# Attention with queries on rows: key sums as backward scans on VectorE, weights transposed on TensorE, own keys and values of two heads in one tile, gating and the final norm rearranged

## The chip, the cores and the metric

The kernel runs on one core of one Trainium2 chip. The metric is the time of one execution on the device in microseconds (us); where several executions are compared, their median. In the lines of the profile, PE is TensorE (PEld its weight loads), DVE is VectorE, ACT is ScalarE, POOL is GpSimd, SP is SyncE, which here only issues transfers.

## The reference, cut to what matters

Two request groups (256 new frames, and 64 further frames of a stream that has 256 cached keys and values) go through one layer with shared weights. All of it is float32.

```python
xn = rmsnorm(x, norm_mix)
q, k, v, u, vs, g = split(xn @ w_in)            # 8 heads x 128; 8 gating groups x 128
z = einsum('bqhd,bkhd->bhqk', q, k) * 128 ** -0.5
mask = k_pos[None, :] < q_pos[:, None]
log_stay = where(mask, log_sigmoid(-z), 0.0)
log_rest = cumsum(log_stay, axis=3, reverse=True) - log_stay
w = where(mask, exp(log_sigmoid(z) + log_rest), 0.0)
a = einsum('bhqk,bkhd->bqhd', w, v)             # sample group: k, v = cached rows, then its own
vs = rmsnorm(gelu(vs), sgu_norm)
bb = gelu(u) * (spatial mix of vs in 128-position chunks + b_spatial)
h = x + (sigmoid(g_a) * (a @ w_a) + sigmoid(g_b) * (bb @ w_b)) @ w_out
hn = rmsnorm(h, norm_ffn)
h = h + (silu(hn @ w_gate) * (hn @ w_up)) @ w_down
y = rmsnorm(h, norm_final)                      # outputs: y, k, v, and vs of the sample rows
```

The sum runs over the keys from the last one backwards. With softplus sp(z) = -log_sigmoid(-z), the weight of a key is exp(z - sum of sp over this key and all later ones).

## The kernel before, in words

**Layout.** Features lie on the 128 partitions, and the 320 positions (256 prompt, 64 sample) along the free dimension. Each large product is done as three float32r products: the weight tile is split into a rounded part `wh` (ScalarE, L75) and a rest `wl` (VectorE, L76), the activations likewise, and `product` (L80 to L85) issues hi*hi, hi*lo and lo*hi for each 128x128 weight block.

**The weight pipeline.** `block` (L87) computes 128 output features: it takes the weights in halves of 8 blocks (1024 columns). A half, here called a chunk, is one transfer of 512 KB issued by SP, one `wh`, one `wl` and 24 matmuls of 320 columns. The pool has 3 raw buffers and 4 pairs of split buffers, so the `wh` of a chunk can only be written when TensorE has finished the chunk four before it, and the transfer of a chunk waits for the `wl` of the chunk three before it. After each chunk a counter, the tick, advances, and functions that were booked for that tick (`at`) put their instructions into the program there. So the attention and gating work is strewn between the chunks of the projections. Each engine runs its own queue in order; which instruction stands where on ScalarE, VectorE and GpSimd is decided when the program is built.

**Attention, in pairs of heads.** `attend` (L442) books for each pair of heads: scores two ticks after its last projection, `att_values` at 4, `att_sums` at 6, `att_out` of the two heads at 9 and 10. Keys lie on the partitions of the score tiles, queries along the free dimension. `att_scores` computes k^T q in full float32 (10 matmuls), copies them out of PSUM with the mask added, and makes the softplus of two tiles of 512 and 640 columns: Abs, Exp, Ln on ScalarE, one VectorE instruction, then a hi and lo split. `att_sums` gets the sums over later keys as products with a triangle and a block of -1 (12 float32r matmuls on `sph` and `spl`), adds the scores and takes Exp. `att_values` transposes v to keys on partitions (6 transposes), and `att_out` multiplies (5 matmuls for each head). The scratch tiles z and e of 640 columns come from the pool of 8 tiles named `D`.

**Gating.** For each of 8 groups: `sgu_turn` scales by the norm and transposes (3 transposes), two ticks later `sgu_mix` does three float32 matmuls with the mask of the chunk, adds the bias and multiplies by u.

**The end.** After the last `w_down` product, L573 adds it to h, L582 squares it, six one-column matmuls (L590) sum the squares of all features, ScalarE takes a square root, VectorE refines the reciprocal in five small instructions (L593, L154 to L157) and writes three diagonal matrices (L598); three matmuls (L599) spread them over all partitions, 16 VectorE instructions (L601) scale the output and 9 transfers (L605) write it.

Of the kernel before, what the change touches and what calls it, by code (L numbers as in the profile page):

```python
# [8 lines left out]
F32 = mybir.dt.float32  # L9
F32R = mybir.dt.float32r  # L10
# [3 lines left out]
P = 128  # L14
# [19 lines left out]
def stream_step(ctx: ExitStack, tc: tile.TileContext, xT, w_in, w_a, w_b, w_out, w_gu, w_down,  # L34
# [93 lines left out]
    def t320(tag, bufs=2, dt=F32):  # L128
# [15 lines left out]
    neg1 = const.tile([P, P], F32, name="neg1")  # L144
    nc.gpsimd.memset(neg1, -1.0)
    negt = const.tile([P, P], F32, name="negt")
    nc.gpsimd.affine_select(out=negt, in_=neg1, pattern=[[-1, P]], base=0, channel_multiplier=1,
                            compare_op=ALU.is_ge, fill=0.0)
    neg1r = const.tile([P, P], F32R, name="neg1r")
    negtr = const.tile([P, P], F32R, name="negtr")  # L150

# [137 lines left out]
    for o, i in ((neg1r, neg1), (negtr, negt)):  # L289
        tc.keep_in_program_order(nc.vector.tensor_copy(o, i))  # L290
# [6 lines left out]
    bsb = apool.tile([P, H, P], F32, name="bsb")  # L297

    def gate_load():
        tc.keep_in_program_order(nc.sync.dma_start(out=wst.rearrange("p g t -> p (g t)"), in_=ws_t))  # L300
        nc.gpsimd.memset(wst[64:128, :, 0:64], 0.0)

    def bias_load():
# [5 lines left out]
    KT1, S0, NA = 512, 768, 1152  # L309
    mask0 = apool.tile([P, 256], F32, name="mask0")  # L310
    nc.gpsimd.memset(mask0, 0.0)

    nc.gpsimd.affine_select(out=mask0, in_=mask0, pattern=[[1, 256]], base=0,
                            channel_multiplier=-1, compare_op=ALU.is_gt, fill=NEG)

    mask2 = apool.tile([P, 64], F32, name="mask2")
    nc.gpsimd.memset(mask2, 0.0)
    nc.gpsimd.affine_select(out=mask2, in_=mask2, pattern=[[1, 64]], base=64,
                            channel_multiplier=-1, compare_op=ALU.is_gt, fill=NEG)
    nc.gpsimd.memset(mask2[0:64, :], NEG)  # L320

    def heads(t, n):
        return t.rearrange("p (h t) -> p h t", h=n)

    def att_load(p):
        s = attn[p]
        s["ck"] = apool.tile([P, 2, PAST], F32, tag="ck", name="ck")
        tc.keep_in_program_order(nc.sync.dma_start(out=s["ck"].rearrange("p h t -> p (h t)"),
                                                   in_=ck_t[:, 2 * p * PAST : (2 * p + 2) * PAST]))
        s["cv"] = apool.tile([P, 2, 2, P], F32, tag="cv", name="cv")  # L330
        tc.keep_in_program_order(nc.sync.dma_start(out=s["cv"].rearrange("p i h d -> p i (h d)"),
                                                   in_=cv[:, :, 2 * p * P : (2 * p + 2) * P]))

    def att_scores(p):
        s = attn[p]
        z0, z1 = aux(), aux()
        zs = [aux(), aux()]
        for j in range(2):
            q, k = s["q", j], s["k", j]
            nc.tensor.matmul(z0[:, j * 256 : (j + 1) * 256], k[:, 0:128], q[:, 0:256], start=True, stop=True)  # L340
            nc.tensor.matmul(z1[:, j * P : (j + 1) * P], k[:, 128:256], q[:, 128:256], start=True, stop=True)
            for i in range(3):
                kk = s["ck"][:, j, i * P : (i + 1) * P] if i < 2 else k[:, 192:320]
                nc.tensor.matmul(zs[j][:, i * P : (i + 1) * P], kk, q[:, 192:320], start=True, stop=True)  # L344
        zm = (pair("zm0")[:, 0:KT1], pair("zm1"))
        for j in range(2):
            nc.vector.tensor_tensor(out=zm[0][:, j * 256 : (j + 1) * 256], in0=z0[:, j * 256 : (j + 1) * 256],
                                    in1=mask0, op=ALU.add)
            nc.vector.tensor_tensor(out=zm[1][:, j * P : (j + 1) * P], in0=z1[:, j * P : (j + 1) * P],
                                    in1=mask0[:, :P], op=ALU.add)  # L350
            to = zm[1][:, 256:].rearrange("p (i h t) -> p i h t", i=3, h=2)[:, :, j, :]
            of = zs[j][:, 0:384].rearrange("p (i t) -> p i t", i=3)[:, :, 64:128]
            nc.vector.tensor_copy(to[:, 0:2, :], of[:, 0:2, :])
            nc.vector.tensor_tensor(out=to[:, 2, :], in0=of[:, 2, :], in1=mask2, op=ALU.add)

        hi = apool.tile([P, NA], F32R, tag="sph", name="sph")
        lo = apool.tile([P, NA], F32R, tag="spl", name="spl")
        for z, r in zip(zm, (slice(0, KT1), slice(KT1, NA))):
            e = pair("e")[:, : r.stop - r.start]
            nc.scalar.activation(out=e, in_=z, func=AF.Abs)  # L360
            nc.scalar.activation(out=e, in_=e, func=AF.Exp, scale=-1.0)
            nc.scalar.activation(out=e, in_=e, func=AF.Ln, bias=1.0)  # L362
            nc.vector.scalar_tensor_tensor(out=e, in0=z, scalar=0.0, in1=e, op0=ALU.max, op1=ALU.add)
            nc.scalar.copy(out=hi[:, r], in_=e)
            nc.vector.tensor_tensor(out=lo[:, r], in0=e, in1=hi[:, r].bitcast(F32), op=ALU.subtract)
        s["zm"], s["sp"] = zm, (hi, lo)

    def att_sums(p):

        s = attn[p]  # L370
        zm = s["zm"]
        c0, c1, c2 = aux(), aux(), aux()
        c0b = heads(c0, 2)[:, :, 128:256]
        for i, sp in enumerate(s["sp"]):
            a, b = i == 0, i == 1
            nc.tensor.matmul(c0, negtr, sp[:, 0:KT1], start=a, stop=False)
            nc.tensor.matmul(c0b, neg1r, heads(sp[:, KT1:S0], 2), start=False, stop=b)
            nc.tensor.matmul(c1[:, 0:256], negtr, sp[:, KT1:S0], start=a, stop=b)
            nc.tensor.matmul(c2[:, 128:512], negtr, sp[:, S0:NA], start=a, stop=False, skip_group_check=True)
            nc.tensor.matmul(c2[:, 128:384], neg1r, sp[:, S0 + P : NA], start=False, stop=False, skip_group_check=True)  # L380
            nc.tensor.matmul(c2[:, 128:256], neg1r, sp[:, S0 + 2 * P : NA], start=False, stop=b, skip_group_check=True)
        w0, w1 = zm
        nc.vector.tensor_tensor(out=w0, in0=c0, in1=w0, op=ALU.add)
        nc.scalar.activation(out=w0, in_=w0, func=AF.Exp)
        nc.vector.tensor_tensor(out=w1[:, 0:256], in0=c1[:, 0:256], in1=w1[:, 0:256], op=ALU.add)
        nc.vector.tensor_tensor(out=w1[:, 256:], in0=c2[:, 128:512], in1=w1[:, 256:], op=ALU.add)
        nc.scalar.activation(out=w1, in_=w1, func=AF.Exp)


    own = {}  # L390
    for name, r in (("att", slice(0, 64)), ("sgu", slice(64, P))):
        own[name] = [apool.tile([P, P], F32, name=f"own_{name}{i}") for i in range(2)]
        for t in own[name]:
            nc.gpsimd.memset(t[r, :], 0.0)

    def turned(src, spans, kind, i):

        pt = aux()
        for k, (t0, n) in enumerate(spans):
            nc.tensor.transpose(pt[:n, k * P : (k + 1) * P], src[:, t0 : t0 + n], ident)  # L400
        vn = apool.tile([P, 2, P], F32, tag="vn", bufs=2, name="vn")
        nc.scalar.copy(out=vn.rearrange("p i d -> p (i d)"), in_=pt[:, 0:256])
        o, r = own[kind][i % 2], slice(64, P) if kind == "att" else slice(0, 64)
        nc.scalar.copy(out=o[r, :], in_=pt[r, 256:384])
        return vn, o

    def att_values(p):
        s = attn[p]
        s["vn"] = [turned(s["v", j], ((0, P), (P, P), (192, P)), "att", j) for j in range(2)]

    def att_out(p, j):
        s = attn[p]
        (w0, w1), (vn, own_v), cvt = s["zm"], s["vn"][j], s["cv"]
        po = aux1()

        lo = 256 - 64 * j
        for i in range(3):
            v = cvt[:, i, j, :] if i < 2 else own_v
            nc.tensor.matmul(po[:, lo : lo + P], v, w1[:, 256 + i * P : 256 + (i + 1) * P],  # L419
                             start=i == 0, stop=i == 2)  # L420
        nc.tensor.matmul(po[:, 0:256], vn[:, 0, :], w0[:, j * 256 : (j + 1) * 256], start=True, stop=False)  # L421
        nc.tensor.matmul(po[:, 128:256], vn[:, 1, :], w1[:, j * P : (j + 1) * P], start=False, stop=True)
        aT[2 * p + j] = split("B", po[:, 0:T])
# [238 lines left out]
```

## Time and profile before

| what | value |
|---|---|
| time, median of 3 runs | 1727.84 us (1725.51 to 1728.11) |
| the profiled execution | 1727.79 us, of which 1726.1 us are the span from first to last instruction |
| mean granted TensorE clock | 0.996 |
| busy share | PE 99%, DVE 50%, ACT 39%, POOL 2% |
| mean transfer rate | 152 GB/s |

The page gives for each group of instructions the line, the engine, what is written from what, the count, the busy time in us, the mean time of one in ns, and the idle time of the engine just before them with what ended it. The chain of waits lists, in order of time, the work that set the end: start, length, what. There a matmul counts with the time until the next one starts; in the timeline it counts from its start to the end of its last column, so neighbours overlap. A full float32 matmul appears as two records (`x2`).

### The profile page before, as it was taken

What the parts mean: (1) busy time and instruction counts of PE and PEld (TensorE: products, weight loads), DVE (VectorE), ACT (ScalarE), POOL (GpSimd) and SP (SyncE); (2) the same over time, 40 slices, a digit from 0 to 9 for tenths busy, and PEclk for the clock granted to TensorE, in tenths of its full rate; (3) what the DMA queues carried; (4) which work ended last, traced back from release to release, by engine and by line L of the source; (5) the groups of instructions that cost most, each with busy time, mean ns of one, the idle gap of its engine ahead of it and who ended that gap; (6) DMA issues with size and microseconds to landing.
All of it is one profiled execution on the core that took longest, in us unless ns stands there. A gap on an engine that the chain in (4) does not pass through costs nothing.

```text
span 1726.1 us, 27576 instructions
## 1 busy us (share of the span) xinstructions
PE 1711.0 (99%) x11670; PEld 1708.0 (99%) x11670; DVE 857.2 (50%) x1087; ACT 677.8 (39%) x838; POOL 40.8 (2%) x66
## 2 busy tenths in 40 slices
PE   9999999999999999999999999999999999999997
PEld 9999999999999999999999999999999999999997
DVE  6654446544444445555444444444444444444455
ACT  6554464433333333444333332233333322333342
POOL 0000011000000000110000000000000000000000
PEclk9999999999999999999999999999999999999998
DMA  7454434344444445554444445444444544444453
GB/s 248 161 179 147 158 127 149 128 153 147 149 153 151 147 149 168 175 169 147 150 154 148 148 151 153 147 147 152 153 147 148 154 151 147 149 155 149 129 152 110
DMA packets 79612, 263.20 MB, mean 152 GB/s; under 512 B 8960, under 2 KB 14080, under 8 KB 79488
## 3 DMA queue, kind: packets, MB, share of 16 engines
q1 hardware_dynamic: 78048, 258.25, 46.1%
q0 software_dynamic: 1024, 2.89, 0.5%
q8 instruction: 91, 1.49, 0.3%
q10 hardware_dynamic: 416, 0.31, 0.1%
q14 instruction: 33, 0.27, 0.0%
HBM read 255.90 MB, written 5.51 MB: 151 GB/s over the span
## 4 chain that ended last, share of the span: by engine, by line
PE 98%; ACT 1%; DVE 1%; DMA 0%; issue 0%; ACTq 0%; DVEq 0%
PE acc L84 31%; PE acc L83 31%; PE acc L85 31%; PE aux L227 2%; PE acc L227 1%; DVE h L601 0%; PE aux L419 0%; PE aux L400 0%; PE aux L344 0%; DMA raw<-w_in 0%; PE aux L421 0%; PE aux L340 0%; ACT L471 0%; ACT L362 0%; DVE wl L76 0%; ACT wh L75 0%
## 5 line engine op out<-in xcount | busy, mean ns | idle before, releaser
L75 ACT CAST wh<-raw 128x1024 fp32r<-128x1024 f32 x468 | 484.4, 1035 | 971.5 <-PE acc L84 801.8
L76 DVE TENSOR_TENSOR wl<-raw,wh 128x1024 fp32r<-128x1024 f32 x468 | 565.1, 1208 | 511.1 <-ACT wh L75 508.5
L83 PE MATMUL acc<-A,wh 128*128 128x320 f32 x2464 | 764.1, 310 | 0.0
L85 PE MATMUL acc<-A,wl 128*128 128x320 f32 x2464 | 761.5, 309 | 0.5 <-DVE wl L76 0.5
L84 PE MATMUL acc<-A,wh 128*128 128x320 f32 x2464 | 761.3, 309 | 0.0
L85 PEld LDWEIGHTS acc<-A,wl 128*128 128x128 f32 x2464 | 462.5, 188 | 0.7 <-DVE wl L76 0.7
L83 PEld LDWEIGHTS acc<-A,wh 128*128 128x128 f32 x2464 | 462.6, 188 | 0.2
L84 PEld LDWEIGHTS acc<-A,wh 128*128 128x128 f32 x2464 | 462.6, 188 | 0.2
L85 PE MATMUL acc<-B,wl 128*128 128x320 f32 x960 | 296.6, 309 | 0.0
L83 PE MATMUL acc<-B,wh 128*128 128x320 f32 x960 | 296.6, 309 | 0.0
L84 PE MATMUL acc<-B,wh 128*128 128x320 f32 x960 | 296.6, 309 | 0.0
L83 PEld LDWEIGHTS acc<-B,wh 128*128 128x128 f32 x960 | 180.2, 188 | 0.0
L84 PEld LDWEIGHTS acc<-B,wh 128*128 128x128 f32 x960 | 180.2, 188 | 0.0
L85 PEld LDWEIGHTS acc<-B,wl 128*128 128x128 f32 x960 | 180.2, 188 | 0.0
L83 PE MATMUL acc<-mh,wh 128*128 128x320 f32 x256 | 79.1, 309 | 0.0
L84 PE MATMUL acc<-ml,wh 128*128 128x320 f32 x256 | 79.1, 309 | 0.0
L85 PE MATMUL acc<-mh,wl 128*128 128x320 f32 x256 | 79.1, 309 | 0.0
L563 DVE TENSOR_TENSOR bb<-acc,rh 128x320 f32<-128x320 f32 x44 | 21.6, 492 | 57.8 <-PE acc L85 57.8
L560 DVE TENSOR_TENSOR ev<-acc,rh 128x320 f32<-128x320 f32 x44 | 21.6, 492 | 56.3 <-PE acc L85 56.3
L573 DVE TENSOR_TENSOR h<-acc,h 128x320 f32<-128x320 f32 x48 | 23.5, 489 | 49.9 <-PE acc L85 49.9
L83 PEld LDWEIGHTS acc<-mh,wh 128*128 128x128 f32 x256 | 48.1, 188 | 0.0
L84 PEld LDWEIGHTS acc<-ml,wh 128*128 128x128 f32 x256 | 48.1, 188 | 0.0
(196 smaller groups left out, 768.0 us busy)
## 6 DMA issues: line engine op xcount, KB each, us to landing
raw<-w_gu SPq DMA_DIRECT2D x176, 512.0 KB, 3.5
raw<-w_in SPq DMA_DIRECT2D x141, 512.0 KB, 3.6
raw<-w_down SPq DMA_DIRECT2D x80, 512.0 KB, 3.5
raw<-w_out SPq DMA_DIRECT2D x32, 512.0 KB, 3.6
raw<-w_a SPq DMA_DIRECT2D x16, 512.0 KB, 3.5
raw<-w_b SPq DMA_DIRECT2D x16, 512.0 KB, 3.5
raw<-w_down SPq DMA_DIRECT2D x16, 256.0 KB, 2.7
xr<-xT SPq DMA_DIRECT2D x16, 160.0 KB, 2.6
```

What stands on the lines that cost most here:

```text
L75: nc.scalar.copy(out=wh[:, : n * P], in_=raw[:, : n * P])
L76: nc.vector.tensor_tensor(out=wl[:, : n * P], in0=raw[:, : n * P], in1=wh[:, : n * P].bitcast(F32), op=ALU.subtract)
L83: nc.tensor.matmul(ps[:, :T], a, x[0], start=first, stop=False)
L84: nc.tensor.matmul(ps[:, :T], a, x[1], start=False, stop=False)
L85: nc.tensor.matmul(ps[:, :T], b, x[0], start=False, stop=last)
L227: nc.tensor.matmul(first[b][h][:, :T], w[:, (h * n + j) * P : (h * n + j + 1) * P], xs[c + j][i], start=not last and c + j + i == 0, stop= ...
L560: nc.vector.tensor_tensor(out=t, in0=pg, in1=got["rh"], op=ALU.mult)
L563: nc.vector.tensor_tensor(out=u, in0=pu, in1=got["rh"], op=ALU.mult)
L573: nc.vector.tensor_tensor(out=hs[m], in0=ps, in1=hs[m], op=ALU.add)
```

## The change

- **Scores.** Queries now lie on the partitions, keys along the free dimension. Scores of the prompt are two matmuls for each head (128 and 256 columns); the 64 sample queries of the two heads are put on partitions 0 to 63 and 64 to 127 of one tile by two matmuls of 320 columns with 64 stationary columns. The cached keys are loaded behind the own keys into one tile `k` (`att_keys`), the cached values by `att_rows`, two ticks after the scores.
- **Sums.** The softplus is no longer split. Six `tensor_tensor_scan` instructions on VectorE (L367) run backwards over 128, 256, 128, 256, 64 and 256 columns; the last starts from the value of the one before. Then z minus the sum, and Exp. `att_sums` with its 12 matmuls is gone, and so are its constants.
- **Turning.** `att_turn`, eight ticks after the scores, transposes 14 blocks of 128x128: four of v, one with the sample values of both heads (`vo`, gathered by two GpSimd copies), and nine of weights. Three ScalarE and two VectorE instructions copy them out.
- **Output.** `att_out` for a pair comes four ticks later: one matmul with the own keys of both heads, four of 64 columns with the cached values, and 256 and 128 columns for each head.
- **Gating** works on pairs of groups: five transposes and five matmuls for two groups (before six and six); the 64 sample positions of both share a tile and a block-diagonal weight tile `wso`, which two GpSimd transfers fill.
- **The end.** The last addition, square and sum are done in two pieces (192 and 128 columns); three one-column matmuls instead of six; GpSimd takes the power -0.5 of three columns; three matmuls with a broadcast of these columns replace the diagonals. `busy` puts 6 and 4 matmuls, whose result is not used, before and behind the one-column matmuls. The last transfer is cut into two.

```diff
+        for j in range(2):
+            nc.tensor.matmul(za[j][:, 0:P], q[:, j, 0:P], k[:, j, 0:P], start=True, stop=True)
+            nc.tensor.matmul(za[j][:, P:Z], q[:, j, P:TP], k[:, j, 0:TP], start=True, stop=True)
+        for j, r in enumerate(ROWS):
+            nc.tensor.matmul(zs[r, 0 : KT - TP], q[:, j, TP:T], k[:, j, TP:KT], start=True, stop=True)
...
+        for j, lo, hi, begin in ((0, 0, P, 0.0), (0, P, Z, 0.0), (1, 0, P, 0.0), (1, P, Z, 0.0),
+                                 (1, Z, Z + TS, 0.0), (0, Z, Z + PAST, es[1][:, Z : Z + 1])):
+            back = es[j][:, lo:hi][:, ::-1]
+            nc.vector.tensor_tensor_scan(out=back, data0=ones[:, 0:1].broadcast_to([P, hi - lo]), data1=back,
+                                         initial=begin, op0=ALU.mult, op1=ALU.add)
+        for zz, e in zip(z, es):
+            nc.vector.tensor_tensor(out=zz, in0=zz, in1=e, op=ALU.subtract)
...
-        for i, sp in enumerate(s["sp"]):
-            a, b = i == 0, i == 1
-            nc.tensor.matmul(c0, negtr, sp[:, 0:KT1], start=a, stop=False)
...
+        for i in range(4):
+            nc.tensor.transpose(cols(bv, i), v[:, i // 2, i % 2 * P : (i % 2 + 1) * P], ident)
+        nc.tensor.transpose(cols(ba, 3), s["vo"], ident)
+        for j, b in enumerate((ba, bb)):
+            for i in range(3):
+                nc.tensor.transpose(cols(b, i), cols(z[j], i), ident)
+        for i in range(2):
+            nc.tensor.transpose(cols(bs_, i), cols(z[0], 3 + i), ident)
+        nc.tensor.transpose(cols(bs_, 2), wown, ident)
...
+        mm(po[0][:, TP : TP + P], av[:, 4 * P :], wt[:, 2 * Z + 2 * P :], True, False)
+        for j, r in enumerate(ROWS):
+            for i in range(2):
+                lo = 2 * Z + i * P + j * TS
+                mm(po[0][:, TP + j * TS : TP + (j + 1) * TS], cvt[:, i, j, :], wt[:, lo : lo + TS], False, i == 1)
+        for j in range(2):
+            mm(po[j][:, 0:TP], av[:, 2 * j * P : (2 * j + 1) * P], wt[:, j * Z : j * Z + TP], True, False)
+            mm(po[j][:, P:TP], av[:, (2 * j + 1) * P : (2 * j + 2) * P], wt[:, j * Z + TP : (j + 1) * Z], False, True)
...
         at(now + 2, att_scores, p)
-        at(now + 4, att_values, p)
-        at(now + 6, att_sums, p)
-        at(now + 9, att_out, p, 0)
-        at(now + 10, att_out, p, 1)
+        at(now + 4, att_rows, p)
+        at(now + 10, att_turn, p)
+        at(now + 14, att_out, p)
...
+                for r in PIECES:
+                    keep(nc.vector.tensor_tensor(out=hs[m][:, r], in0=ps[:, r], in1=hs[m][:, r], op=ALU.add))
+                    nc.scalar.activation(out=last[:, r], in_=hs[m][:, r], func=AF.Square)
+                for r in PIECES:
+                    keep(nc.vector.tensor_tensor(out=last[:, r], in0=last[:, r], in1=sqf.total[:, r], op=ALU.add))
...
+    busy(6)
     ps = aux1()
     for t0, c in spans:
+        keep(nc.tensor.matmul(ps[:, c], last[:, t0 : t0 + P], ones[:, 0:1], start=True, stop=True))
...
+    nc.gpsimd.tensor_tensor(out=r, in0=ms, in1=mhalf, op=ALU.pow)
+    busy(4)
...
+        keep(nc.tensor.matmul(rf[:, t0 : t0 + P], r[:, c].to_broadcast([P, P]), ident, start=True, stop=True))
```

VectorE, softplus of the first pair before: `zm` are the masked scores, `e` the softplus, `spl` its rest for the sums, `wl` the rest of a weight chunk, `v` and `k` evictions of projections.

```order
L354 TENSOR_TENSOR zm_796<-aux,mask_622 128x64
L363 SCALAR_TENSOR_TENSOR e<-zm_795,e 128x512
L76 TENSOR_TENSOR wl<-raw,wh 128x1024
L365 TENSOR_TENSOR spl<-e,sph 128x512
L363 SCALAR_TENSOR_TENSOR e<-zm_796,e 128x640
L433 TENSOR_TENSOR v<-acc,rx 128x320
L76 TENSOR_TENSOR wl<-raw,wh 128x1024
L365 TENSOR_TENSOR spl<-e,sph 128x640
```

The same place now: `z` are the scores, `e` the softplus, and L367 the scans (their operand `ones` is the factor of one).

```order
L360 SCALAR_TENSOR_TENSOR e<-z_775,e 128x640
L360 SCALAR_TENSOR_TENSOR e<-z_776,e 128x448
L367 SCALAR_TENSOR_TENSOR e<-ones,e 128x128
L367 SCALAR_TENSOR_TENSOR e<-ones,e 128x256
L367 SCALAR_TENSOR_TENSOR e<-ones,e 128x128
L367 SCALAR_TENSOR_TENSOR e<-ones,e 128x256
L367 SCALAR_TENSOR_TENSOR e<-ones,e 128x64
L428 TENSOR_TENSOR v<-acc,rx 128x320
L367 SCALAR_TENSOR_TENSOR e<-ones,e 128x256
L370 TENSOR_TENSOR z_776<-z_776,e 128x448
L370 TENSOR_TENSOR z_775<-z_775,e 128x640
L76 TENSOR_TENSOR wl<-raw,wh 128x1024 x3
```

Where a `wl` stood between the steps of the softplus, the next `wl` now stands behind the whole run of softplus, scans and subtractions.

TensorE, sums of the first pair before (this half is for `sph`; the same six follow for `spl`):

```order
L376 MATMUL aux<-sph,negtr 128x512
L377 MATMUL aux<-sph,neg1r 128x2x128
L378 MATMUL aux<-sph,negtr 128x256
L379 MATMUL aux<-sph,negtr 128x384
L380 MATMUL aux<-sph,neg1r 128x256
L381 MATMUL aux<-sph,neg1r 128x128
```

TensorE now, transposes of the first pair, which stand four chunks later in the program than the sums did:

```order
L383 MATMUL aux<-ident,v 128x128 x4
L384 MATMUL aux<-ident,vo 128x128
L387 MATMUL aux<-ident,z_775 128x128 x3
L387 MATMUL aux<-ident,z_776 128x128 x3
L389 MATMUL aux<-ident,z_775 128x128 x2
L390 MATMUL aux<-ident,wown 128x128
```

The 12 sums are gone and 14 transposes (with v's six of before among them) stand in one place, eight chunks behind the scores instead of two and four.

TensorE at the end of the program now, behind the last product (`col` are the three columns of the norm):

```order
L85 MATMUL acc<-B,wl 128x320
L586 MATMUL aux<-h,ones 128x128 x6
L628 MATMUL aux_16392<-ones,last 128x1 x3
L586 MATMUL aux<-h,ones 128x128 x4
L635 MATMUL aux<-ident,col_16397 128x128 x3
```

Before, six one-column matmuls L590 and the three of L599 stood there, with nothing between or ahead of them.

More of the change, by code (lines that the diff above doesn't have):

```diff
@@ L143, in stream_step @@
     nc.gpsimd.memset(ones, 1.0)
[L144 to L150, printed above, removed]
     def newton(r, ms, e):
@@ L320, in stream_step @@
[L320 to L331, printed above, removed]
+    Z, KT = 384, T + PAST
@@ L335, in att_scores @@
         s = attn[p]
-        z0, z1 = aux(), aux()
-        zs = [aux(), aux()]
+        q, k = s["q"], s["k"]
+        za, zs = (aux(), aux()), aux()
         for j in range(2):
[L339 to L344, printed above, removed]
@@ L361, in att_scores @@
+        es = []
+        for zz in z:
+            e = pair("e")[:, : zz.shape[1]]
+            nc.scalar.activation(out=e, in_=zz, func=AF.Abs)
             nc.scalar.activation(out=e, in_=e, func=AF.Exp, scale=-1.0)
             nc.scalar.activation(out=e, in_=e, func=AF.Ln, bias=1.0)
-            nc.vector.scalar_tensor_tensor(out=e, in0=z, scalar=0.0, in1=e, op0=ALU.max, op1=ALU.add)
-            nc.scalar.copy(out=hi[:, r], in_=e)
-            nc.vector.tensor_tensor(out=lo[:, r], in0=e, in1=hi[:, r].bitcast(F32), op=ALU.subtract)
@@ L390, in stream_step @@
[L390 to L423, printed above, removed]
+            nc.vector.scalar_tensor_tensor(out=e, in0=zz, scalar=0.0, in1=e, op0=ALU.max, op1=ALU.add)
@@ new lines, in att_out @@
+    def att_out(p):
+        s = attn.pop(p)
+        wt, av, cvt = s["wt"], s["av"], s["cv"]
+        po = aux1(), aux()
+        mm = lambda out, a, b, first, last: nc.tensor.matmul(out, a, b, start=first, stop=last, skip_group_check=True)
+        mm(po[0][:, TP : TP + P], av[:, 4 * P :], wt[:, 2 * Z + 2 * P :], True, False)
[6 more added lines that the diff above has]
+            mm(po[j][:, P:TP], av[:, (2 * j + 1) * P : (2 * j + 2) * P], wt[:, j * Z + TP : (j + 1) * Z], False, True)
+        aT[2 * p] = split("B", po[0][:, 0:T])
+        hi, lo = aT[2 * p + 1] = slot("B"), slot("B")
+        for r, src in ((slice(0, TP), po[1][:, 0:TP]), (slice(TP, T), po[0][:, T : T + TS])):
+            nc.scalar.copy(out=hi[:, r], in_=src)
+            nc.vector.tensor_tensor(out=lo[:, r], in0=src, in1=hi[:, r].bitcast(F32), op=ALU.subtract)
@@ new lines, in sgu_turn @@
+    def sgu_turn(p):
+        pt, po = aux(), aux()
+        for i in range(4):
+            nc.tensor.transpose(pt[:, i * P : (i + 1) * P], vs[2 * p + i // 2][:, i % 2 * P : (i % 2 + 1) * P], ident)
+        nc.tensor.transpose(po[:, 0:P], vown.pop(p), ident)
+        t = apool.tile([P, 5 * P], F32, tag="av", name="vsn") if p % 2 else apool.tile([P, 3 * Z], F32, tag="wt", name="vsn")
+        vn = vnat[p] = t[:, 0 : 5 * P].rearrange("p (i d) -> p i d", i=5)
+        nc.scalar.copy(out=vn[:, 0:4].rearrange("p i d -> p (i d)"), in_=pt)
+        nc.scalar.copy(out=vn[:, 4], in_=po[:, 0:P])
+        if p + 1 < H // 2:
+            sgu_gain(p + 1)
@@ L553, in stream_step, with busy @@
     last = const.tile([P, T], F32, name="last")
+    mhalf = const.tile([P, 3], F32, name="mhalf")
+    nc.gpsimd.memset(mhalf, -0.5)
+    PIECES = (slice(P, T), slice(0, P))
+    keep = tc.keep_in_program_order
+    def busy(n):
+        d = aux()
+        for _ in range(n):
+            keep(nc.tensor.matmul(d[:, 0:P], ones, hs[0][:, 0:P], start=True, stop=True))
     for s0, n in SLICES:
@@ L587, in stream_step @@
+    spans = ((192, slice(2, 3)), (128, slice(1, 2)), (0, slice(0, 1)))
+    busy(6)
     ps = aux1()
     for t0, c in spans:
-        for i, t in enumerate((sqf.total, last)):
-            nc.tensor.matmul(ps[:, c], t[:, t0 : t0 + P], ones[:, 0:1], start=i == 0, stop=i == 1)
-    ms, r, e = (const.tile([P, 3], F32, name=f"col{i}") for i in range(3))
-    nc.scalar.activation(out=r, in_=ps[:, 0:3], func=AF.Sqrt, bias=eps_t, scale=1.0 / D)
+        keep(nc.tensor.matmul(ps[:, c], last[:, t0 : t0 + P], ones[:, 0:1], start=True, stop=True))
```

178 lines of the change are left out of this document (98 added, 80 removed).

## The prediction

> **What bounds the kernel now.** I read the page first, then the chain of waits around each step that the change touches, then groups by line and shape, and the timeline of one pair.
>
> ```profile
> span 1726.1 us, 27576 instructions
> PE 1711.0 (99%) x11670; PEld 1708.0 (99%) x11670; DVE 857.2 (50%) x1087; ACT 677.8 (39%) x838; POOL 40.8 (2%) x66
> PE 98%; ACT 1%; DVE 1%; DMA 0%; issue 0%; ACTq 0%; DVEq 0%
> L85 PE MATMUL acc<-A,wl 128*128 128x320 f32 x2464 | 761.5, 309 | 0.5 <-DVE wl L76 0.5
> ```
>
> TensorE is busy for 99% of the span and is 98% of the chain; the others have half their time free. So an instruction that leaves TensorE gives its issue time back, and work on VectorE, ScalarE, GpSimd or in transfers costs nothing until TensorE waits for it. The last row shows one such wait, 0.5 us in all; the change must not make more of them. The last stretch, where TensorE has run dry, counts on its own.
>
> The profiled execution took 1727.79 us, 1.7 more than its span, and stands on the median of 1727.84. I work against 1727.79 and leave the 1.7 alone. 0.2% (3.5 us) is about what a measurement can tell from no change.
>
> **TensorE between the chunks.** The chain gives what each step adds to the stream, here for the second pair and one gating group.
>
> ```profile
> 107.87 0.43 PE aux L340 x2
> 108.30 0.22 PE aux L341 x2
> 108.52 0.67 PE aux L344 x6
> 110.52 0.15 PE acc L83
> 117.56 0.66 PE aux L400 x6
> 125.25 0.23 PE aux L376
> 127.16 0.15 PE acc L84
> 137.57 0.67 PE aux L419 x6
> 138.24 0.43 PE aux L421 x2
> 138.67 0.22 PE aux L422 x2
> 280.44 0.22 PE aux L491 x2
> 281.11 0.33 PE aux L400 x3
> 46.62 0.54 PE aux L163 x2
> ```
>
> Prices: a float32 matmul takes 0.43 us at 256 columns, 0.22 at 128, 0.54 at 320; a 128-column transpose 0.11. Before, a pair costs 2.65 for scores (107.87 to 110.52), 0.66 for values, 1.76 for sums (125.25 to 127.16, less one 0.15 of the stream) and 2 x 1.32 for outputs (0.67 + 0.43 + 0.22): 7.71.
>
> Now: scores 2 x (0.43 + 0.22) + 2 x 0.54 = 2.38. Transposes 14 x 0.11 = 1.54. Outputs: one matmul of 128 columns 0.22, for each head 0.65, and four of 64 columns. If columns set the price those cost 0.11 each; but the end of the kernel has float32 matmuls of one column:
>
> ```profile
> 1712.01 0.36 PE L590 MATMUL aux<-ones,sq_f 128*128 128x1 f32 x2
> 1712.23 0.36 PE L590 MATMUL aux<-ones,last 128*128 128x1 f32 x2
> ```
>
> They start 0.22 apart, like 128 columns, so loading 128 stationary columns sets a floor; I take 0.22 and keep 0.11 for the lower end. Outputs are 0.22 + 4 x 0.22 + 1.30 = 2.40, the pair 6.32: 1.39 less, 5.6 us for four pairs (7.3 with the cheap end).
>
> No row shows two matmuls of 64 stationary columns in different halves of the output. Row: a group of three gating transposes takes 0.33, and its third has 64 stationary columns, so that costs the usual 0.11. [...] If the two 0.54 overlap wholly, 2.2 us are won. [...]
>
> Gating: a group costs 3 x 0.22 + 0.33 = 0.99, eight 7.9. Now each of four pairs has 5 x 0.22 + 5 x 0.11 = 1.65, 6.6 in all: 1.3 less.
>
> Two waits go with the sums: that of the fourth pair for a late `wl` (0.5 above), and this one:
>
> ```profile
> L377 PEld LDWEIGHTS aux<-spl,neg1r 128*128 128x128 f32 x4 | 0.8, 189 | 0.3 <-DVE spl L365 0.3
> ```
>
> 0.8 together, since the operand `spl` is no more. What is late next is the subject of the next part. So far: 5.6 + 1.3 + 0.8 = 7.7 us.
>
> **What hides the new VectorE work.** The scans cost nothing as long as `wl` comes in time, because TensorE has chunks in hand. VectorE's queue is strict, so behind softplus, scans and subtractions stand all `wl`; TensorE waits for those.
>
> ```profile
> 64.65 1.04 ACT L75 CAST wh<-raw 128x1024 fp32r<-128x1024 f32 x1 [2.47 <-PE acc L84]
> 66.87 0.42 DVE L347 TENSOR_TENSOR zm<-aux,mask 128x256 f32<-128x256 f32 x1
> 67.20 0.28 DVE L349 TENSOR_TENSOR zm<-aux,mask 128x128 f32<-128x128 f32 x1
> L363 DVE SCALAR_TENSOR_TENSOR e<-zm,e 128x640 f32<-128x640 f32 x4 | 3.3, 826 | 3.2 <-ACT e L362 3.2
> L154 DVE RECIPROCAL rx<-rx 128x320 f32<-128x320 f32 x1 | 2.2, 2153 | 0.6 <-ACT rx L168 0.6
> L76 DVE TENSOR_TENSOR wl<-raw,wh 128x1024 fp32r<-128x1024 f32 x452 | 554.2, 1226 | 511.0 <-ACT wh L75 508.5 <-PE acc L227 2.3
> L433 DVE TENSOR_TENSOR v<-acc,rx 128x320 f32<-128x320 f32 x6 | 2.9, 488 | 5.0 <-PE acc L85 5.0
> L361 ACT ACTIVATE e<-e 128x640 f32<-128x640 f32 x4 | 3.0, 738 | 0.0
> L362 ACT ACT_TABLE_LOAD x8 | 10.3, 1283 | 0.1
> ```
>
> A VectorE instruction costs about 1.07 ns an element (0.42 at 256, 0.83 at 640) plus 0.15, and the next starts 0.08 before it ends (66.87, 67.20); so 128, 64, 448 columns are 0.28, 0.22, 0.63. ScalarE takes 0.65 from start to start at 640 and, at the 0.8 ns an element between L361 and the 1.04 of `wh`, 0.49 at 448.
>
> First pair, from t = 0 where the scores start. The `wh` of the fourth chunk ahead is written at once, as at 64.65. VectorE: evictions from 0.85 with a `wl` among them, 0.33 + 0.20 + 1.15 + 0.33 + 0.20 + 0.14 + 0.34, to 3.5. ScalarE: Abs, Exp, Ln on both tiles, 3 x 1.14, and two table loads 2.56, to 9.6. VectorE: softplus to 10.4, six scans, 1088 elements at 1.07 plus 0.07 each, 1.6, the eviction of v 0.4, subtractions 1.3, `wl` 1.2: ready at 14.9. TensorE needs it after the scores (2.38), four chunks of 24 x 0.147 (14.1) and two matmuls (0.3): 16.8. Margin 1.9. By the same sum the second pair, whose deadline lies 2.4 later through the outputs and which waits for the casts of those outputs, has 4.1; the third, where a `wl` stands ahead of the last scan, 5.2; the fourth 3.2. No wait, no cost.
>
> No row shows a scan. The nearest is L363 (two inputs, two operations), 1.07 ns an element, which I take; the slowest in VectorE's table is the reciprocal, 6.3. [...]
>
> Costed at nothing, with their cover: copies out of the transposes (two chunks, 7 us, before the outputs need them); the two transfers of the sample weights and the GpSimd copies of v (POOL 2% busy); the key load, same bytes. The value load waits in SP's queue for the outputs of the pair before, with weight transfers behind it; so it does already, and the transfer behind it needs a `wl` that now comes later than the outputs in any case:
>
> ```profile
> SPq L331 <- PE aux L419: 7.8, 3, 2.7
> ```
>
> **The end.**
>
> ```profile
> 1710.72 0.50 DVE h L573
> 1711.24 0.48 ACT last L582
> 1711.76 1.29 PE aux L590 x10
> 1714.58 1.66 PE aux L599 x6
> 1716.26 2.08 DVE h L601 x5
> L137 POOL MEMSET eps_t<- 128x1 f32 x1 | 0.1, 99 | 0.3 <-POOLq L645 0.3
> L183 POOL TENSOR_TENSOR sq_v<-sq_v,sq 128x320 f32<-128x320 f32 x7 | 7.2, 1023 | 59.2 <-ACT sq L182 59.2
> y_t<-h SPq DMA_DIRECT2D x7, 320.0 KB, 2.3
> y_t<-h SPq DMA_DIRECT2D x2, 160.0 KB, 1.8
> ```
>
> Now the first piece (192 columns: 0.35 on VectorE, 0.37 on ScalarE) is added, squared and summed by 1711.9, the second runs beside it. Three matmuls start 0.22 apart and the last ends 0.36 after its start: 1712.7. VectorE's scaling of three columns (0.15 by the formula above) ends at 1712.9. GpSimd's power has no row: between a fill of one column (0.10) and an addition of 320 (1.02); three columns are nearer the first, I take 0.3. The four unused matmuls occupy TensorE until 1713.4 anyway. Three matmuls at 0.22 instead of 0.55 (if the clock holds), last end at +0.80: the output scaling starts at 1714.3 instead of 1716.26, 2.0 us sooner (1.4 with 1.02 for the power). The last transfer has half the bytes: 0.5. Together 2.5.
>
> **Sum.** 7.7 + 2.5 = 10.2; 1727.8 - 10.2 = 1717.6.
>
> **Rivals.**
> *Late weights at the scans, partly.* VectorE's run in the four pairs is longer than I sum, since a scan costs two to three times L363's price an element (1.2 to 2.3 us a pair) and a dozen instructions that depend on each other overlap less (0.1 to 0.2 us each): then the first pair waits 1 to 2 us and the fourth up to 1 or 2: 1719 to 1722. For it: before, the same place already made TensorE wait 0.5. Against: the margins. [...]
> *Scans at the reciprocal's rate, 6.3 ns.* 5.7 us more a pair (4.4 ahead of the third's `wl`): waits of 3.8, 1.6, 0 and 2.5, 7.9 in all: 1725.5, no change that can be told.
> *Slower.* The same place, VectorE's scans ahead of `wl`, still slower: four pairs lose about 4100 elements times the excess over 1.07, less 14.4 of margin. It eats the gain and 3.5 us more from 8 ns an element; at 10 ns it loses 22, giving 1740. For it: a scan needs each result for the next element, which no row here does, and runs backwards. Against: no VectorE row is that slow.
> *The cheap end:* 64 columns at 0.11 and overlapping halves: 1.8 + 2.2 more, 1713.6.
>
> **How the numbers follow.** Forecast, with its own range 1714.5 to 1719: 0.70. Partly late weights 0.15, both faster. Cheap end 0.03, faster. Reciprocal's rate 0.08, same. Slower 0.04. That makes faster 0.88, same 0.08, slower 0.04. The range 1714.5 to 1722 takes in one of the two cheap bounds, the drain, the slow power and the partly late weights, and leaves out some 0.15 to 0.2.
>
> **What would show it.** Right: no idle time of TensorE behind `wl` beyond 1 us; scores, transposes and outputs at 2.4, 1.5 and 2.4 a pair; 3.5 to 4 us from the last product to the output scaling. Wrong: scan rows above 2.5 ns an element with `wl` as releaser of L85; the two sample score matmuls starting far from 0.54 apart; the 64-column output matmuls at 0.11; idle time of TensorE ahead of the transposes or outputs of a pair, or of the gating transposes, which would mean that the tick distances don't cover the new chain; a GpSimd row above 1 us at the end.

## The result, and the profile after

The changed kernel takes 1718.16 us, median of 6 runs (1716.78 to 1718.74), against 1727.24 (1725.51 to 1728.11, 6 runs) for the kernel before on the same chip. The ratio is 0.9947, 95% interval 0.9937 to 0.9957: faster by 0.53%. The forecast was 1717.6, with 1714.5 to 1722.0 as its range.

The profiled execution took 1716.78 us, the quickest of the six. Page of the changed kernel:

```profile
span 1715.0 us, 27450 instructions
PE 1702.2 (99%) x11616; PEld 1696.7 (99%) x11616; DVE 861.9 (50%) x1097; ACT 658.8 (38%) x819; POOL 46.1 (3%) x73
```

TensorE is as full as before, with 8.8 us less to do; VectorE's share is unchanged, since the scans replaced splits and additions. Three intervals of the traces divide the program better than the time does. In the five kernels below that leave the middle as it is, it comes out at 1637.27 each time, so a difference of 0.1 there means something.

| us | before | after | gained |
|---|---|---|---|
| start of the span to the first score matmul | 64.60 | 62.82 | 1.78 |
| middle: first score matmul to the start of the last L85 | 1645.77 | 1637.27 | 8.50 |
| last L85 to the first output scaling (L601, L637) | 5.90 | 4.58 | 1.32 |
| first output scaling to the end of the span | 9.82 | 10.32 | -0.50 |

The change doesn't touch the first row, which differs from run to run (the experiment warm_9). Without it the traces give 9.3 us, and the medians differ by 9.08.

The second pair's scores in the chain of waits, then the first pair's transposes and outputs, and one gating step (times in us from the start of the span, length, engine, line, pieces):

```profile
101.90 0.22 PE aux L342 x2
102.12 0.43 PE aux L343 x2
102.56 0.22 PE aux L342 x2
102.78 0.43 PE aux L343 x2
103.21 0.69 PE aux L345 x4
103.90 0.34 PE acc L83
...
93.34 0.44 PE aux L383 x4
93.78 0.11 PE aux L384
93.88 0.66 PE aux L387 x6
94.54 0.22 PE aux L389 x2
94.76 0.11 PE aux L390
...
111.14 2.42 PE aux L403 x18
...
278.72 0.22 PE aux L503 x2
278.94 0.89 PE aux L505 x8
279.83 0.44 PE aux L490 x4
280.27 0.11 PE aux L491
```

Transposes 1.54, outputs 2.42 and gating 1.66 are the prices of the prediction (1.54, 2.40, 1.65). The scores are not: the two matmuls of 64 stationary columns (L345) take 0.69, and the first chunk matmul behind them 0.34 instead of 0.15. That is 0.88 for both where the prediction had 2 x 0.54.

The first pair on VectorE, and the matmul on TensorE that needs the first `wl` behind the scans (timelines):

```profile
72.33 1.36 DVE L360 SCALAR_TENSOR_TENSOR e<-z,e 128x640 f32<-128x640 f32 x2 [5.84 <-ACT e L359]
73.61 2.08 DVE L367 TENSOR_TENSOR_SCAN e<-ones,e 128x128 f32<-128x128 f32 x5
75.61 0.46 DVE L428 TENSOR_TENSOR v<-acc,rx 128x320 f32<-128x320 f32 x1
75.99 0.74 DVE L367 TENSOR_TENSOR_SCAN e<-ones,e 128x256 f32<-128x256 f32 x1
76.65 1.33 DVE L370 TENSOR_TENSOR z<-z,e 128x448 f32<-128x448 f32 x2
77.90 3.49 DVE L76 TENSOR_TENSOR wl<-raw,wh 128x1024 fp32r<-128x1024 f32 x3
```

```profile
79.39 0.31 PE L85 MATMUL acc<-A,wl 128*128 128x320 f32 x1
```

The first of the three `wl` is done at 79.12 and needed at 79.39: the margin is 0.27 us, where the prediction had 1.9. Of the 1.6 that are missing, 1.0 is the scans' price, 0.4 a softplus that ended later than summed, and 0.2 the cheaper scores, which bring the need for `wl` forward. Counted in the same way, chunk by chunk, the other pairs have 3.1, 4.9 and 2.5 (predicted 4.1, 5.2 and 3.2). No wait for `wl` is left in the trace.

The end, from the timeline:

```profile
1700.44 0.56 DVE L609 TENSOR_TENSOR h<-acc,h 128x192 f32<-128x192 f32 x2 [3.40 <-PE acc L85]
1701.64 0.83 PE L628 MATMUL aux<-ones,last 128*128 128x1 f32 x6
1702.75 0.89 POOL L631 TENSOR_TENSOR col<-col,mhalf 128x3 f32<-128x3 f32 x1 [929.22 <-DVE col L630]
1703.69 0.93 PE L635 MATMUL aux<-ident,col 128*128 128x128 f32 x6 [0.22 <-POOL col L631]
1704.67 6.45 DVE L637 TENSOR_TENSOR h<-h,aux 128x320 f32<-128x320 f32 x16 [2.00 <-PE aux L635]
```

The three matmuls of L635 take 0.93 where the prediction had 0.80, and the power on GpSimd takes 0.89 and not 0.3.

### The profile page after: what moved, and what is told of

Read it like the earlier page. It is cut to its first block, busy times and chain, and to the rows that moved or that the text cites. A ratio compares the mean times of both kernels' runs of the same rounds, so it can differ in the third digit from the quotient of the medians.

```text
span 1715.0 us, 27450 instructions
## 1 busy us (share of the span) xinstructions
PE 1702.2 (99%) x11616; PEld 1696.7 (99%) x11616; DVE 861.9 (50%) x1097; ACT 658.8 (38%) x819; POOL 46.1 (3%) x73
## 4 chain that ended last, share of the span: by engine, by line
issue 54%; PE 45%; DVE 0%; DMA 0%; ACT 0%; POOL 0%; POOLq 0%; ACTq 0%; DVEq 0%
PE acc L83 13%; PE acc L84 13%; PE acc L85 13%; PE aux L219 2%; PE acc L219 1%; PE aux L403 1%; DVE h L637 0%; DMA raw<-w_in 0%; PE aux L505 0%; PE aux L343 0%; PE aux L345 0%; PE aux L387 0%; PE aux L342 0%; PE aux L490 0%; PE aux L383 0%
## 5 line engine op out<-in xcount | busy, mean ns | idle before, releaser
L85 PE MATMUL acc<-A,wl 128*128 128x320 f32 x2464 | 761.5, 309 | 0.0
L85 PEld LDWEIGHTS acc<-A,wl 128*128 128x128 f32 x2464 | 462.6, 188 | 0.0
L85 PE MATMUL acc<-B,wl 128*128 128x320 f32 x960 | 296.6, 309 | 0.0
L85 PEld LDWEIGHTS acc<-B,wl 128*128 128x128 f32 x960 | 180.2, 188 | 0.0
L85 PE MATMUL acc<-mh,wl 128*128 128x320 f32 x256 | 79.1, 309 | 0.0
L85 PEld LDWEIGHTS acc<-mh,wl 128*128 128x128 f32 x256 | 48.0, 188 | 0.0
```

The source lines that it names most:

```text
L85: nc.tensor.matmul(ps[:, :T], b, x[0], start=False, stop=last)
```

## The experiments

The theory after the two traces: the gain is TensorE instructions that left, 7 us in the attention and 1.3 in the gating, plus 0.8 at the end, where the power and the transfers give back most of what the rest wins; the scans are hidden, with little margin. The main rivals: the gain comes from the end or the start and not from the attention; or VectorE's cover is wide and its margins mean nothing.

### One part undone at a time

Three kernels are the changed one with one part as it was before: the attention (with its constants `neg1`, `negt`), the gating (`sgu_turn`, `sgu_mix` by groups, no `wso`), and the end (from the last product on).

> The changed kernel with the attention of before: sums on TensorE, one head at a time; gating and end stay new. Theory: the attention carries most of the gain, through TensorE instructions that left. By the rows of the two profiles a pair cost 7.71 us before and costs 2.19 for scores (two matmuls of 64 stationary columns overlap in part) + 1.54 for transposes + 2.42 for outputs = 6.15 after: 6.2 us for four pairs, and .8 of waits come back: about 7.0 slower than the changed kernel's 1718.2, 1725.2. From the first scores to the last product of the chunks some 1644 us instead of 1637.1. The prediction's own terms give 6.4, so 1724.6. Rival: the gain lies in the end and in a sooner start of TensorE's full clock, and the attention's part is small: 1721 or less.

> The changed kernel with the gating of before, one group at a time, three matmuls and three transposes each. Theory: eight groups at .99 us against four pairs at 1.66 (.22 + .89 + .44 + .11): 1.3 us more, 1719.5, and 1638.4 us from the first scores to the last product of the chunks. Rival: the gating transposes wait for nothing and hide nothing, but its evictions on VectorE delay weights, so that more than 1.3 comes back.

> The changed kernel with the end of before: column sums from two operands, square root and one Newton step, diagonals, the last transfer whole, no unused matmuls. Theory from the two profiles: from the last product to the end of the span 15.73 us before and 14.91 after, so .8 us more, 1719.0. Rival, the prediction's term: 2.5 us more, 1720.7. Then the profile of the changed kernel had a slow end by chance.

| | median us (runs) | middle | last L85 to scaling | scaling to end |
|---|---|---|---|---|
| changed kernel | 1718.16 (6) | 1637.27 | 4.58 | 10.32 |
| old_attention | 1725.54 (11) | 1644.49 | 4.57 | 10.32 |
| old_gating | 1719.19 (5) | 1638.57 | 4.57 | 10.30 |
| old_end | 1719.14 (5) | 1637.27 | 5.90 | 9.81 |

The attention is worth 7.22, the gating 1.30, the end 0.82 (1.33 won, 0.51 lost): 9.34, against 9.32 for the whole difference of the traces behind the first scores. The parts add up and each moves its own interval alone. The runs of the experiments come from three chips, on which the median of the kernel before was 1726.45 to 1727.45, so the intervals carry the argument and not the medians. The rival that the attention's part is small falls. Both waits are back with the old attention, as long as before: 0.3 for `spl`, and this one for `wl` (TensorE's groups by line):

```profile
L85 PE MATMUL acc<-A,wl 128*128 128x320 f32 x2464 | 761.6, 309 | 0.5 <-DVE wl L76 0.5
```

### The scans' cover

no_scans drops the loop of scans, so the sums along the keys are left out; scans_2 puts an unused forward scan ahead of each; abs_5 lengthens the work ahead of the scans on ScalarE:

```
-            nc.scalar.activation(out=e, in_=zz, func=AF.Abs)
+            for _ in range(5):
+                nc.scalar.activation(out=e, in_=zz, func=AF.Abs)
```

> The changed kernel without the six scans of each pair; softplus is left in their place, so the sums along the keys are not computed. Theory: the scans stand beside TensorE's chunks and end .3 us or more before TensorE needs what is queued behind them, so they cost nothing: 1637.3 us from the first scores to the last product of the chunks, as with them, and 1718.2 in all. [...]

> The changed kernel with a second, unused scan ahead of each of the six, over the same softplus into a spare tile, forwards; those of 128 columns take their ones from a whole tile, the others by broadcast as before. That is 2.8 us more a pair on VectorE at the changed kernel's rows. VectorE's order changes: in the first pair a wl now stands ahead of the second scan and two more among the scans, so it should be there some 2.5 us sooner than in the changed kernel. Theory: no wait, 1637.3 us from the first scores to the last product. Rival: VectorE's block is the limit whatever its order, and 2.5 us of wait appear. For the price: if running backwards or broadcasting the ones made a scan slow, the spare rows are near .42 us for 256 and .28 for 128 columns, like other VectorE rows; if the scan itself is slow, they are .69 and .41 as in the changed kernel.

> The changed kernel with each Abs of the attention done five times in place (same numbers): 4 more of 640 and of 448 columns on ScalarE, some 4.6 us a pair, ahead of softplus, scans and subtractions and so of the next wl. VectorE's order of instructions changes a little: the first pair's wl moves ahead of the eviction of v, the last scan and the subtractions (2.3 us), the fourth's ahead of one eviction (.4). Theory: TensorE has a chunk's wl ready .3, 3.1, 4.9 and 2.5 us before it needs it in the four pairs of the changed kernel's trace, and nothing else hides a later one. So waits of 4.6 - 2.3 - .3 = 2.0, 1.3, 0 and 4.6 - .4 - 2.5 = 1.7: 5.0 in all, 1723.2, with VectorE's wl as releaser of TensorE's wait. With the margins of the prediction (1.9, 4.1, 5.2, 3.2): .4 + .5 + 0 + 1.0 = 1.9, 1720.1. Rival: VectorE and ScalarE are only half busy, so that 4.6 us more a pair stay hidden: 1718.2.

no_scans: 1718.53 us median of 4, middle 1637.62. Nothing is gained. It is even 0.35 longer: VectorE's order came out otherwise in the fourth pair, where a `wl` now ends as TensorE needs it, as in the kernel before.

scans_2: 1717.76 us median of 4, middle 1637.27. The 2.8 us a pair vanish, since the `wl` moved ahead among the scans. Its groups of scans (the row L372 is the changed kernel's own, L370 the spare one; busy us, mean ns):

```profile
L372 DVE TENSOR_TENSOR_SCAN e<-ones,e 128x256 f32<-128x256 f32 x12 | 8.4, 704 | 0.1
L370 DVE TENSOR_TENSOR_SCAN spare<-ones,e 128x256 f32<-128x256 f32 x12 | 8.0, 664 | 0.0
L372 DVE TENSOR_TENSOR_SCAN e<-ones,e 128x128 f32<-128x128 f32 x8 | 3.4, 419 | 0.1
L370 DVE TENSOR_TENSOR_SCAN spare<-ones,e 128x128 f32<-128x128 f32 x8 | 3.3, 408 | 0.0
```

Forwards or backwards, with ones from a whole tile or by broadcast, a scan of 128 or 256 columns costs the same within 6%: (692 - 409) / 128 = 2.2 ns an element in the changed kernel, twice the 1.07 of L363 before. So the scan itself is slow, and neither its direction nor the broadcast makes it so.

abs_5: 1723.45 us median of 11, middle 1643.76, so 6.5 us of waits or what follows from them, where 5.0 were expected. TensorE's wait row and the rows around the fourth pair's wait (timeline; then windows with PE and PEld busy, DVE, ACT, POOL, granted TensorE clock, DMA share, GB/s):

```profile
L85 PE MATMUL acc<-A,wl 128*128 128x320 f32 x2464 | 762.5, 309 | 3.4 <-DVE wl L76 3.4
```

```profile
223.96 0.41 PE L85 MATMUL acc<-A,wl 128*128 128x320 f32 x1 [2.08 <-DVE wl L76]
```

```profile
222.00:224.00 2.00, 0.04 (x1) 0.05 (x1) 2.00 (x4) 1.94 (x6) 0.00 (x0) 1.00 0.00 0
224.00:225.00 1.00, 1.00 (x5) 1.00 (x6) 0.30 (x1) 1.00 (x1) 0.00 (x0) 0.66 0.16 33
225.00:226.00 1.00, 1.00 (x6) 1.00 (x5) 0.00 (x0) 0.99 (x3) 0.00 (x0) 0.50 0.72 266
226.00:227.00 1.00, 1.00 (x5) 1.00 (x5) 0.30 (x1) 1.00 (x3) 0.00 (x0) 0.50 0.58 225
227.00:228.00 1.00, 1.00 (x6) 1.00 (x6) 0.93 (x1) 1.00 (x3) 0.89 (x1) 0.63 0.00 0
```

From one chunk's first `wl` to the next, against the changed kernel, TensorE loses 1.85 us in the first pair, 0.7 in the second, nothing in the third and 2.24 in the fourth: 4.8 for the 2.0, 1.3, 0 and 1.7 expected. So the margins are real, and the cover is not wide: both the rival (nothing) and the prediction's margins (1.9 us of waits) fall.

The fourth pair's loss has a second part, which the expectation didn't have. Its last scan took 1.42 us, where the changed kernel's take 0.74 or 0.75, while GpSimd ran an addition for the gating beside it (timelines):

```profile
220.10 1.42 DVE L368 TENSOR_TENSOR_SCAN e<-ones,e 128x256 f32<-128x256 f32 x1
220.09 0.88 POOL L175 TENSOR_TENSOR sq_v<-sq_v,sq 128x320 f32<-128x320 f32 x1 [21.93 <-ACT sq L174]
```

The only other scan of these traces that stands beside this addition, one of 64 columns in scans_2, took 0.96 instead of 0.27. So 0.67 of the 2.24 goes with this overlap, which leaves 1.57 for the 1.7 expected; no run takes the addition away.

The other 1.7 come from the clock. It falls to a half behind the longest wait and stays there for 3.4 us (what the last four windows lack, 0.34 + 0.50 + 0.50 + 0.37, at a half), in which matmuls start 0.27 apart and not 0.15. A loss of 2.24 us was enough for the fall, and one of 1.85 was not: the clock reads 1.00 all through the first pair's wait, which one matmul at 81.63 divides. No run looks for the limit between the two, or for what sets the 3.4 us.

### The two half-width score matmuls

scores_apart only changes the order, so that no two matmuls of 64 stationary columns stand together:

```
+        for j, r in enumerate(ROWS):
             nc.tensor.matmul(za[j][:, 0:P], q[:, j, 0:P], k[:, j, 0:P], start=True, stop=True)
+            nc.tensor.matmul(zs[r, 0 : KT - TP], q[:, j, TP:T], k[:, j, TP:KT], start=True, stop=True)
             nc.tensor.matmul(za[j][:, P:Z], q[:, j, P:TP], k[:, j, 0:TP], start=True, stop=True)
```

> The changed kernel with the two score matmuls of 64 stationary columns apart: each stands between the two full-width ones of its head, so that they are never next to each other. Theory: next to each other they took .89 us because the second starts in the other half of the output while the first still runs; apart each costs the .54 of 320 columns, so .19 more a pair, .8 in all: 1638.0 us from the first scores to the last product. Rival: 64 stationary columns are cheaper by themselves, at .45, and nothing changes: 1637.3. If changing between full and half width drained TensorE, it would show as more than .8, since there are now four changes a pair in place of two.

It took 1722.00 us, median of 6, with a middle of 1640.77: 3.50 us more, 0.88 a pair, not 0.19. The chain of its second pair, second head (L343 is the half-width matmul here, L344 the one of 256 columns):

```profile
106.30 0.22 PE aux L342 x2
106.53 0.68 PE aux L343 x2
107.21 0.63 PE aux L344 x2
```

A lone half-width matmul takes 0.68, and the 256 columns behind it 0.63 instead of 0.43: 0.14 and 0.20 more than their columns, 0.34 in all. Two together cost 0.88 (0.69, and 0.19 more on the chunk matmul behind), which is 0.54 + 0.34: the second is free. In the changed kernel's trace its two passes start 0.005 to 0.007 us after the first one's, in all four pairs. So two things hold at once: the whole overlap, which the prediction had as its cheap end, and a price beyond the columns, 0.34 for each stay at half width (one stay a pair in the changed kernel, two here). No run shows whether the change of width is what costs it. The two passes of a lone half-width float32 matmul start 0.32 apart, not 0.27 (half of 0.54), so part of the price may lie in the matmul itself. The row that the prediction set beside this, a transpose with 64 stationary columns in before's gating that costs the usual 0.11, shows neither; why a transpose is spared was not tried.

### The end, and the start

> The changed kernel without the ten unused matmuls at the end. Theory: TensorE then stands idle 1.4 us and 1.2 us in its last five, its granted clock falls to half as it did at the end of the kernel before, and the last three matmuls take .55 instead of .22 each: .7 us more from the last product to the output scaling (5.3 instead of 4.58). Rival: the clock doesn't fall in so short a stretch: 4.6, and the unused matmuls did nothing.

> The changed kernel with a multiplication in place of the power on GpSimd at the end, so that the output's scale is not computed; the time of this one row is looked for. Theory: the power is what takes .89 us on three columns, and a multiplication takes .3 or less, so the output scaling starts .6 sooner, 4.0 us after the last product instead of 4.58. Rival: any instruction of GpSimd with two tensor operands takes some .9 at so few columns: 4.58.

no_busy leaves out `busy(6)` and `busy(4)`: 1717.20 us, median of 4, and 5.00 us from the last product to the scaling, 0.43 more. Its last three matmuls, and the windows over them (columns as above):

```profile
1703.85 1.36 PE L633 MATMUL aux<-ident,col 128*128 128x128 f32 x6 [1.23 <-POOL col L630]
```

```profile
1704.00:1704.50 0.50, 0.50 (x4) 0.50 (x5) 0.00 (x0) 0.00 (x0) 0.00 (x0) 0.69 0.00 0
1704.50:1705.00 0.50, 0.50 (x4) 0.41 (x2) 0.00 (x0) 0.00 (x0) 0.00 (x0) 0.50 0.00 0
```

The clock falls in the middle of them, where the changed kernel's trace has 1.00 throughout, and they take 1.36 for its 0.93. So the unused matmuls do hold the clock; since it falls a little later than expected, 0.4 and not 0.7 is lost. A median doesn't show 0.4 here, the interval does.

pool_mult has `op=ALU.mult` for `op=ALU.pow`, so the output's scale is left out; it ran once, in 1716.52 us. Its row of GpSimd, from the timeline:

```profile
1703.00 0.20 POOL L631 TENSOR_TENSOR col<-col,mhalf 128x3 f32<-128x3 f32 x1 [929.22 <-DVE col L630]
```

The power is the expensive part: 0.89 against 0.20 for a multiplication of the same shape. The row is 0.69 shorter, the scaling starts 0.49 sooner (4.09 after the last product): the unused matmuls of `busy(4)` are then the last to end ahead of L635.

> The changed kernel with 9 instead of 7 unused matmuls at the start, nothing else. It is on the spread, not on the change: in some traces (before, old_attention, old_end, abs_5) the first matmuls of 320 columns after the unused ones are .31 us apart until about 9 us, in others (the changed kernel, no_busy) .15 from the start, and the first scores start some 1.6 to 2.0 us sooner. Theory: a wait of 1.0 to 1.5 us between the unused matmuls and the first weights lets TensorE's rate fall back, by chance; two more fill .96 us of that wait, so all runs are of the sooner kind: median 1716.8 instead of 1718.2, first scores at 62.8. Rival: the spread comes from the transfers, and the median stays at 1718.2.

> The changed kernel with three edits: 9 unused matmuls at the start; the square root on ScalarE with its table loaded ahead and a reciprocal on VectorE in place of the power on GpSimd; the last transfer whole. Theory: first scores at 62.8 in all runs; power and the instruction before it (1.18 us from the column sums to the last matmuls) give way to .6, so 4.0 us from the last product to the output scaling instead of 4.58; from there to the end 9.8 instead of 10.33, since the transfers are at their full rate from 3 us on and half a last transfer only adds an issue. Together 1716.8 - .6 - .5 = 1715.7. Rival, the prediction's view of the end: the last transfer's half size gains .5, so that whole it costs .5 and the end stays as it is: 1716.7.

The two kinds of start, in the kernel before and in the changed one (timelines):

```profile
5.65 2.50 PE L227 MATMUL acc<-A,wh 128*128 128x320 f32 x8 [1.04 <-ACT wh L217]
9.02 1.81 PE L227 MATMUL aux<-A,wh 128*128 128x320 f32 x8
```

```profile
5.54 1.76 PE L219 MATMUL acc<-A,wh 128*128 128x320 f32 x8 [1.02 <-ACT wh L209]
7.72 1.34 PE L219 MATMUL aux<-A,wh 128*128 128x320 f32 x8
```

Eight matmuls take 2.50 in one and 1.76 in the other, though both waited 1.0 for the first weights: 1.8 us that have nothing to do with the change. In the slower row the matmuls start 0.27 apart, as at half the clock in abs_5. The traces' records of the granted clock divide the starts: the first record of the full clock lies at 4.74 us in the changed kernel and at 10.07 in the one before, and in all 13 traces either by 5.1 us, with the first scores at 62.8 to 63.7, or at 8.8 and later, with the first scores at 64.1 to 64.9. The later group holds kernels whose edits lie behind the first scores (no_scans, old_end), so the kind of start is not the change's doing. What makes the clock rise sooner or later stays open: warm_9 took 1717.03 us, with all 5 runs between 1716.55 and 1717.28, where the changed kernel's six reach from 1716.78 to 1718.74. That fits the theory that two more unused matmuls make every run one of the sooner kind, but best_w below has the same start and spreads over 2.3 us again, and its first scores stand at 63.67 where 62.8 was expected.

best_w combines three edits:

```
-WARM = 7
+WARM = 9
...
-    nc.vector.tensor_scalar(out=ms, in0=ps[:, 0:3], scalar1=1.0 / D, scalar2=EPS, op0=ALU.mult, op1=ALU.add)
-    nc.gpsimd.tensor_tensor(out=r, in0=ms, in1=mhalf, op=ALU.pow)
+    nc.scalar.activation(out=ms, in_=ps[:, 0:3], func=AF.Sqrt, bias=eps_t, scale=1.0 / D)
+    nc.vector.reciprocal(out=r, in_=ms)
...
-    for n in (1, 1, 2, 2, 2, 2, 2, 2, 1, 1):
+    for n in (1, 1, 2, 2, 2, 2, 2, 2, 2):
```

It took 1716.58 us, median of 5 (1715.65 to 1717.95), ratio to before 0.9938 (0.9925 to 0.9950). Its end is 13.89 instead of 14.90 us, 0.49 from the power and 0.52 from the whole last transfer, near the 0.6 and 0.5 expected. The times of this kernel and of the changed one overlap, so the gain stands on the intervals, not on the medians.

That a whole last transfer is quicker than two halves was seen twice (10.30 to 10.33 in every kernel with halves, 9.81 and 9.80 in the two without). The windows of the changed kernel behind the first scaling at 1704.67, columns as above:

```profile
1708.00:1709.00 1.00, 0.00 (x0) 0.00 (x0) 1.00 (x3) 0.00 (x0) 0.00 (x0) 0.50 1.04 394
...
1712.00:1713.00 1.00, 0.00 (x0) 0.00 (x0) 0.00 (x0) 0.00 (x0) 0.00 (x0) 0.50 0.98 359
```

The DMA engines are full from some 3 us behind the first scaling until 2 us after VectorE's last row. The last transfer's bytes queue behind the others', and whole or cut in two they land within 0.09 us of each other (below): nothing is won.

Why 0.5 is lost stands in the trace's records of SyncE, which waits at the end for the semaphores of all transfers. These are its waits there (SyncE's waits; changed kernel, then old_end: us in all, times, longest):

```profile
SPq L684 <- DMA y_t<-h: 1.8, 1, 1.8
SPq L671 <- DMA y_t<-h: 1.5, 2, 0.8
```

In us behind the first scaling, the last transfer lands at 8.99 in the changed kernel and at 8.90 in old_end, only 0.09 sooner. SyncE goes through the semaphores one after the other, 0.06 apart, in the same order in both. In old_end that of the last transfer comes last, so the others are passed while it still runs, and SyncE goes on at 8.98. In the changed kernel the tenth transfer has a semaphore that stands third in this order: SyncE is held there until 9.00, has seven more to go through, and goes on at 9.50. That is the 0.5. best_w, with the whole transfer, goes on at 8.98 as well; no run changes the order alone.

## Why the prediction was right, and where it was off

**What bounds the kernel** held: TensorE's stream. 8.5 of 9.3 us come out of the middle.

**Attention, 5.6 and 0.8 for the waits.** Measured 7.22 for both. Transposes and outputs came as priced; the floor of 0.22 for the 64-column output matmuls, taken from one-column matmuls at the end, was right (the four take 0.84). The mis-sized term is 2 x 0.54 for the sample scores: 0.88, which is 0.8 us more in four pairs. The whole overlap of the cheap end, 2.2 us, came, less the 0.34 a pair beyond the columns, 1.4 in all. The drain that the range takes in is shown by no run; in its place the runs showed these 0.34, without their cause. The price and the overlap apply at once, and 2.2 - 1.4 = 0.8 is the difference; the prediction had no case with both.

**Gating, 1.3.** Measured 1.30.

**The cover of the scans.** The sum didn't need the scan's price, and that held: leaving the scans out gains nothing. The price was wrong by a factor of two, taken from a row of another operation: 1.07 ns an element, where the scans took 2.2. No row of before gave the rival *late weights, partly* its two to three times that price; the scans showed about two. Its near end (1.2 us more a pair, which leaves 0.7 of the first margin's 1.9) was what happened in VectorE's work; the first margin fell to 0.27 and the wait just didn't come. abs_5 shows what more would have cost, and with the clock's fall and GpSimd's addition more than the rival counted. The rivals with scans at 6 to 10 ns fall with the row.

**The end, 2.5.** Measured 0.8: the largest error. Of the 2.0 to the scaling 1.3 came; the power at 0.89 is nearer to the other end that the prediction kept (1.02, with 1.4 sooner). The 0.5 for half a last transfer was wrong in sign: it priced one transfer by its own row, not by the queue in front of it nor by the waits behind it.

Together: 0.8 too little in the middle and 1.7 too much at the end, so 1717.6 came close to 1718.16 partly because two errors cancelled, and partly because it was worked from 1727.8, 0.6 above the median of before that stands beside the result (1727.24). That is luck. Of the signs that it named, two speak against it: the two sample score matmuls took 0.88 together, not 0.54 each, and the output scaling came 4.58 us after the last product, not 3.5 to 4.

## What to carry to other kernels

When TensorE bounds a kernel, moving sums to an idle engine pays by the TensorE issue time that leaves (7.22 us here, with two waits), if the strict queue of the engine that takes them still delivers the weights in time: compute the margin for the earliest deadline, and count a missed one nearly double where it also drops the clock, as the wait of 2.24 us did here. Look as well at what GpSimd runs beside the scans (one took 1.42 us instead of 0.75 here). Where a price and an overlap pull opposite ways, as 0.34 and 0.54 us a pair did here, ask whether both apply before choosing. At the end of a program look at whether the transfers are already at their full rate before cutting the last of them, and at what one more transfer adds to the waits behind it.

## What was not expected of the hardware

- Two half-width float32 matmuls side by side cost 0.88 us, one alone 0.88 too: 0.34 beyond its columns, and the second is free.
- Behind a wait that cost 2.24 us in mid-stream TensorE's clock was halved for 3.4 us; behind those of 1.85 and 0.7 it wasn't.
- A scan of 256 columns took 1.42 us instead of 0.75 while a GpSimd addition of 320 columns ran beside it.
- A power of three columns takes 0.89 us on GpSimd, a multiplication 0.20.
- Ten unused matmuls at the end save 0.43 us: the granted clock is 1.00 with them and falls to 0.50 without.
- One more transfer at the end cost 0.5 us for the same output: SyncE was held until 9.00 us behind the first scaling at the third of its waits and had seven more to go through.
